# Both borders of a three-sublayer encoder trunk in one ordered list of steps

## The chip, the cores and the metric

One core of one Trainium2 chip runs the kernel. The metric is the device time in microseconds of one execution. A core has five engines with a queue of instructions each: TensorE (PE in the profile; its weight loads are PEld), VectorE (DVE), ScalarE (ACT), GpSimd (POOL) and SyncE (SP), which here only issues DMAs. Each engine runs its own queue in order, and engines wait for one another by semaphores.

## The reference

The kernel computes one layer of three sublayers on x of 512 positions by 1024 features, all in float32:

```python
def sublayer(h_res, j, fn, res_w):
    h = rms_norm(h_res, norm_g[l, 2 * j]) * (1.0 + scale) + shift      # scale, shift, gate: from silu(c) @ w_ada
    y = rms_norm(fn(h), norm_g[l, 2 * j + 1])
    return h_res + res_w * gate * y
...
x = sublayer(x, 0, lambda h: swiglu(h, ffn1_w_in[l], ffn1_w_out[l]), 0.5)     # 1024 -> 2 x 2816 -> 1024
x = sublayer(x, 1, mixer, 1.0)
x = sublayer(x, 2, lambda h: swiglu(h, ffn2_w_in[l], ffn2_w_out[l]), 0.5)
```

The mixer is one input projection, four heads of differential attention with rotary embedding, a bidirectional gated linear recurrence with a short convolution, and one output projection.

## The kernel before

Everything lies transposed: features on the 128 partitions, the 512 positions along the free axis, so x is eight tiles `X[:, k]` of 128x512. Each float32 operand of a product is split into a rounded part and the rest (`h` and `l`, "high" and "low"), and each product is three matmuls (`mm3`, lines 155 to 157): high x high, low weight x high, high weight x low. A weight unit comes by DMA from SP into one of three buffers `st` (`wdma`, L177), ACT copies its high part (`wcopy`, L184: `wh`), and DVE or POOL subtracts it for the low part (`wlow`, L192: `wl`). Each of `st`, `wh` and `wl` has three buffers, so unit i waits for unit i-3.

The two FFNs walk over 44 input tiles (`tile`, eight contraction tiles k each) and then over eight output tiles. The eighth output tile is run in two halves of 256 positions (`last_tile`), so that the work that follows can begin with the first half. What follows is a border between two sublayers:

- the norm of the sublayer's output: a Square of the last tile (L895), two small matmuls against ones (`acc` L901, `norm` L905) and a square root on ACT (L906), giving `s1`;
- the residual: x is multiplied by `s1` (L420 on POOL for k = 2 to 7, L422 on DVE for k = 0 and 1) and the gated output `F[k]` is added (L424, and L455 for whole tiles). The residual is kept scaled by `s1`; the factor is carried along (`old`, L909) and taken out later (`rr`, `restore_x`);
- the next sublayer's first products run on the unnormalized x times the scale column: `u_hi` (ACT L411) and `u_lo` (DVE L414) split it, `do_k` multiplies contraction tile k into seven PSUM banks (21 products of three). `early` runs tile 0 on the first half, `begin` tiles 0 and 1 in halves and 2 and 3 whole, `rest` tiles 4 to 7. `shift_cols` (L397) adds the product with the shift as a column;
- the next pre-norm: Squares of X on ACT (L465) summed by POOL (L467), one matmul pair (`do_stats`, L471 and L472), then variance (L511 or, in the mixer, L999), a square root on ACT, and a reciprocal on DVE (L517, L1009) give `r12`. With it X is normalized (L526, L1013) and split into `R.h`, the input of all further tiles, and the seven first products are scaled when they leave PSUM (L772, L1046).

The order of all this is the order in which the Python code is written (`half`, `early`, `begin`, `rest`, and the start of `ffn` for the second FFN). The mixer between is different: `MIXER` is a list of 565 step names, worked off one after another. Each step is a small function (`xs.0`: first evacuation; `cd.0`, L1301 and L1305: a convolution; `cl.0`, L964: its low part; `ga.00`: its gate product; `sc`, scores; `mo`, `mp`: output projection; a suffix `.p` puts a step on POOL). The list begins with the fifth contraction tile of the mixer's input (`kk.4`) and ends with the sum of the output's squares (`pa.6`), and so contains neither border.

## Time and profile before

| | |
|---|---|
| median of 3 runs | 1009.28 us (1006.93 to 1009.36) |
| profiled execution | 1004.12 us, span 1002.3 us |
| PE busy, 0 to 376 us (first FFN) | 367.73 us |
| PE busy, 376 to 429 us (first border) | 48.78 of 53 us |
| PE busy, 429 to 530 us (mixer, first part) | 93.27 of 101 us |
| PE busy, 530 to 606 us (mixer, rest) | 76.00 of 76 us |
| PE busy, 606 to 670 us (second border) | 57.81 of 64 us |
| PE busy, 670 to 1002 us (second FFN) | 318.21 of 332 us |
| mean granted TensorE clock | 0.989 |

Busy time counts a matmul from its start to its modelled end. The granted clock is the share of full speed that TensorE was allowed; where it is under 1, busy time is slow time. The profiled execution was shorter than the three timed runs.

### The profile page before, as it was taken

How to read it: one execution, taken by the hardware profiler on the slowest of the kernel's cores; microseconds unless marked ns; L12 is line 12 of the kernel's file. 1: busy time of each engine (PE TensorE's matmuls, PEld its weight loads, DVE VectorE, ACT ScalarE, POOL GpSimd, SP SyncE). 2: the span in 40 equal slices, each digit the busy share in tenths (PEclk: the TensorE clock that was granted, in tenths of full speed). 3: DMA queues.
4: the chain of work that ended last, by engine and by line, in shares of the span. 5: the costliest groups of instructions: out<-in, count | busy, mean ns of one | idle time of the engine just before them, and what ended most of it. 6: DMA issues, size and time to landing. Idle time of an engine off the chain costs nothing.

```text
span 1002.3 us, 11743 instructions
## 1 busy us (share of the span) xinstructions
PE 961.8 (96%) x4480; PEld 789.3 (79%) x4480; DVE 608.2 (61%) x789; ACT 430.9 (43%) x666; POOL 222.3 (22%) x163
## 2 busy tenths in 40 slices
PE   6999999999999999979999998999999999999994
PEld 5888888888888888767677788778888888888884
DVE  7967655556666648998998647987433333322226
ACT  6653323335222224689878764363332322222230
POOL 1008200000001015612585416644100000001014
PEclk9999999999999999999999999999999999999997
DMA  8846555455687852322320322314233232333312
GB/s 329 291 154 227 191 192 205 177 208 203 217 276 250 284 168 65 93 74 77 90 75 22 82 81 74 100 64 123 88 105 102 87 105 87 93 95 99 95 37 84
DMA packets 45002, 137.10 MB, mean 137 GB/s; under 512 B 7185, under 2 KB 9745, under 8 KB 44946
## 3 DMA queue, kind: packets, MB, share of 16 engines
q1 hardware_dynamic: 44082, 135.62, 41.1%
q8 instruction: 35, 0.57, 0.2%
q10 hardware_dynamic: 864, 0.74, 0.2%
q14 instruction: 21, 0.17, 0.1%
HBM read 132.14 MB, written 2.10 MB: 134 GB/s over the span
## 4 chain that ended last, share of the span: by engine, by line
PE 84%; DVE 7%; ACT 3%; issue 2%; POOL 2%; DMA 1%; SPq 0%; DVEq 0%; ACTq 0%; POOLq 0%
PE PS L157 27%; PE PS L155 27%; PE PS L156 27%; PE PS L1173 1%; PE PS L702 1%; POOL s L526 1%; DVE X L424 1%; DMA q<-in_w_ada 1%; DVE wl L192 1%; DVE s L1565 1%; ACT s L1186 1%; POOL s L467 1%; DVE s L414 1%; PE PS L1210 1%; DVE X L422 1%
## 5 line engine op out<-in xcount | busy, mean ns | idle before, releaser
L155 PE MATMUL PS<-s,wh 128*128 128x512 f32 (+1 forms) x1032 | 395.8, 384 | 1.9 <-ACT s L411 1.4
L156 PE MATMUL PS<-s,wl 128*128 128x512 f32 (+1 forms) x1032 | 392.4, 380 | 2.9 <-POOL wl L192 1.5
L157 PE MATMUL PS<-s,wh 128*128 128x512 f32 (+1 forms) x1032 | 392.5, 380 | 2.1 <-DVE s L414 2.1
L192 DVE TENSOR_TENSOR wl<-st,wh 128x1024 fp32r<-128x1024 f32 (+3 forms) x151 | 189.0, 1253 | 193.8 <-ACT wh L184 193.6
L155 PEld LDWEIGHTS PS<-s,wh 128*128 128x128 f32 x1032 | 194.3, 188 | 41.7 <-ACT s L411 1.8
L156 PEld LDWEIGHTS PS<-s,wl 128*128 128x128 f32 x1032 | 194.4, 188 | 41.7 <-POOL wl L192 2.4
L157 PEld LDWEIGHTS PS<-s,wh 128*128 128x128 f32 x1032 | 194.3, 188 | 39.8 <-DVE s L414 2.7
L184 ACT ACTIVATE wh<-st 128x1024 fp32r<-128x1024 f32 (+2 forms) x170 | 169.8, 1002 | 120.0 <-PE PS L157 109.0
L155 PE MATMUL PS<-q,wh 128*128 128x512 f32 (+1 forms) x288 | 106.5, 370 | 0.0
L156 PE MATMUL PS<-q,wl 128*128 128x512 f32 (+1 forms) x288 | 106.2, 369 | 0.0
L157 PE MATMUL PS<-q,wh 128*128 128x512 f32 (+1 forms) x288 | 106.0, 368 | 0.0
L879 POOL TENSOR_TENSOR s<-s,s 128x512 f32<-128x512 f32 x12 | 15.7, 1308 | 401.1 <-ACT s L875 401.1
L237 DVE CUSTOM_DVE_ANT_0 q<-q,q 128x1024 bf16<-128x1024 f32 x72 | 89.8, 1247 | 0.2 <-DMA q<-in_w_ada 0.2
L793 DVE TENSOR_TENSOR s<-s,PS 128x512 f32<-128x512 f32 x41 | 28.1, 686 | 62.7 <-PE PS L157 62.1
L788 ACT ACTIVATE s<-PS 128x512 f32<-128x512 f32 x40 | 23.8, 595 | 97.6 <-PE PS L157 97.5
L155 PEld LDWEIGHTS PS<-q,wh 128*128 128x128 f32 x288 | 54.3, 189 | 9.7
L156 PEld LDWEIGHTS PS<-q,wl 128*128 128x128 f32 x288 | 54.2, 188 | 9.6
L157 PEld LDWEIGHTS PS<-q,wh 128*128 128x128 f32 x288 | 54.1, 188 | 9.5
L750 ACT ACTIVATE q<-s 128x512 fp32r<-128x512 f32 x28 | 17.7, 631 | 95.8 <-DVE s L793 94.5
L192 POOL TENSOR_TENSOR wl<-st,wh 128x1024 fp32r<-128x1024 f32 (+2 forms) x18 | 39.6, 2205 | 60.1 <-ACT wh L184 60.1
L750 ACT ACTIVATE s<-s 128x512 fp32r<-128x512 f32 x16 | 10.1, 632 | 70.5 <-DVE s L793 70.5
L751 DVE TENSOR_TENSOR q<-s,q 128x512 fp32r<-128x512 f32 x28 | 22.0, 786 | 20.0 <-ACT q L750 20.0
(235 smaller groups left out, 946.6 us busy)
## 6 DMA issues: line engine op xcount, KB each, us to landing
q<-in_w_ada SPq DMA_DIRECT2D x72, 512.0 KB, 4.0
st<-in_w2b SPq DMA_DIRECT2D x37, 512.0 KB, 3.3
st<-in_w1b SPq DMA_DIRECT2D x36, 512.0 KB, 4.5
st<-in_w1o SPq DMA_DIRECT2D x16, 512.0 KB, 4.4
st<-in_w2o SPq DMA_DIRECT2D x16, 512.0 KB, 3.5
st<-in_wma SPq DMA_DIRECT2D x16, 448.0 KB, 4.2
st<-in_w2a SPq DMA_DIRECT2D x16, 448.0 KB, 3.4
st<-in_wmb SPq DMA_DIRECT2D x9, 512.0 KB, 3.7
```

The lines of the kernel that those rows point to most:

```text
L155: PE.matmul(o, wh, ah, start=start, stop=False)
L156: PE.matmul(o, wl, ah, start=False, stop=False)
L157: PE.matmul(o, wh, al, start=False, stop=stop)
L184: ACT.activation(h[:, :n], staged[i][:, :n], AF.Copy)
L192: eng.tensor_tensor(out=l[:, :n], in0=st[:, :n], in1=h[:, :n].bitcast(F32), op=ALU.subtract)
L237: DVE.tensor_tensor_reduce(out=junk, in0=t, in1=cond, op0=ALU.mult, op1=ALU.add, scale=1.0, scalar=0.0, accum_out=ada[:, i:i + 1])
L414: DVE.scalar_tensor_tensor(out=ul[k][:, c], in0=X[:, k, c], scalar=colA(j, k), in1=f32(uh[k][:, c]), op0=ALU.mult, op1=ALU.subtract)
L750: ACT.activation(h, t, AF.Copy)
L751: DVE.tensor_tensor(out=l, in0=t, in1=f32(h), op=ALU.subtract)
L788: ACT.activation(t, PS[:, b], AF.Silu)
L793: DVE.tensor_tensor(out=g, in0=g, in1=PS[:, b], op=ALU.mult)
L879: POOL.tensor_tensor(out=st["acc"], in0=st["acc"], in1=t, op=ALU.add)
```

## The change

Both borders become steps of the list, which grows from 565 to 878 names and now runs from the last output tile of the first FFN (`ws.-5`, `pt.1.0.0`) to the second of the two input tiles after the second FFN's first seven (`tt.8.1`). The functions `half`, `early`, `begin` and `rest` go, and `last_tile` serves only the last sublayer; each instruction of the borders is a step with the border's number (1 or 2), the half (0, 1) and the tile k: `pt` (part of the last output tile), `qs` (its Square), `sa` and `sn` (the norm's matmuls), `sq` (square root), `so` (product of the carried factors), `xm` (x times `s1`, a half), `xf` and `xg` (the added output, half and whole), `uh` and `ul` (the split), `kq` and `kk` (products of contraction tiles 0 and 1 in halves, and of the rest), `sx` and `sax` (Square and sum), `e2` (epsilon term), `sh` and `sw` (shift), `ss` (matmuls of the sum), `hm`, `hf`, `hh`, `hl` (normalized input), `sg`, `sl`, `pg`, `ph`, `pl` (the second FFN's first groups), `tt` (its next two tiles). The steps inside the mixer keep their instructions, but the whole list stands in another order, and which of the steps run on POOL is chosen anew. The side work of the first FFN is packed into 57 places instead of 60.

```diff
 MIXER = """
-wd.2 ws.2 kk.4 kk.5 gh.1 wd.3 gh.0 sd sf sr rv hm.0 ws.3 hf.0 wl.2 hm.2 wl.3 hm.7 hh.0 hm.6 dq hl.0 wd.4 kk.6
...
+ws.-5 lt.1 dq pt.1.0.0 sa.1.0 wl.-5.p pt.1.0.1 pt.1.0.2 pt.1.1.0 qs.1.0 sn.1.0 pt.1.1.1 pt.1.1.2 wd.-4 wd.-3
...
-        def half(F, s1, c):
-
-            for k in range(2, 8):
-                POOL.tensor_tensor(out=X[:, k, c], in0=X[:, k, c], in1=s1[:, c], op=ALU.mult)
-            for k in range(2):
-                DVE.tensor_tensor(out=X[:, k, c], in0=X[:, k, c], in1=s1[:, c], op=ALU.mult)
-            for k in range(2):
-                DVE.tensor_tensor(out=X[:, k, c], in0=X[:, k, c], in1=F[k][:, c], op=ALU.add)
-                u_hi(k, c)
-            for k in range(2):
-                u_lo(k, c)
...
+        def xm(e, b, h, k):
+            c = HF[h]
+            e.tensor_tensor(out=X[:, k, c], in0=X[:, k, c], in1=B["s1", 1][:, c], op=ALU.mult)
+
+        def xf(e, b, h, k):
+            c, f = HF[h], ST[b]["F"][k]
+            e.tensor_tensor(out=X[:, k, c], in0=X[:, k, c], in1=f[:, c], op=ALU.add)
...
+        def sax(e, b, k):
+            t, o = B.pop(("sx", b, k)), B["sx", b, 0]
+            e.tensor_tensor(out=o, in0=o, in1=t, op=ALU.add)
...
-    def mixer(R, s1, nxt, early):
-        base = pos["i"]
+    def trunk(st0, part0, done0, side3, finish, last):
+
+        base = pos["i"] + 7
...
-        for i in range(60):
+        for i in range(57):
...
-        G = group0(1, 7)
-        st = ffn(0, R, side2, step(G), G.early)
...
-        G.begin(st["F"], st["s1"])
...
-        R, G = G, group0(2, 7)
-        st = mixer(R, st["s1"], step(G), G.early)
...
-        G.begin(st["F"], st["s1"])
...
-        G.rest(2)
...
+        st = next(ffn(0, R, side2))
...
+        trunk(st, st["part"], st["done"], side3, finish, last)
```

Three places show how the instructions move. A row names the line, the operation, what it writes and reads (a number tells buffers apart) and the size; `x4` is four in a row. On DVE at the first border, from the last weights of the first FFN (768 wide) on, there stood before:

```order
L192 TENSOR_TENSOR wl<-st,wh 128x768
...
L422 TENSOR_TENSOR X<-X,s_2635 128x256 x2
L424 TENSOR_TENSOR X<-X,s_1991 128x256
L424 TENSOR_TENSOR X<-X,s_2101 128x256
L414 SCALAR_TENSOR_TENSOR s_2754<-X,aA,s_2753 128x256
L414 SCALAR_TENSOR_TENSOR s_2758<-X,aA,s_2757 128x256
L192 TENSOR_TENSOR wl<-st,wh 128x896 x2
```

Now, with L891 for `xm`, L214 for a weight's low part, L438 for `ul` and L901 for `xg`:

```order
L214 TENSOR_TENSOR wl<-st,wh 128x1024
L891 TENSOR_TENSOR X<-X,s_2645 128x256 x4
L214 TENSOR_TENSOR wl<-st,wh 128x896 x2
L438 SCALAR_TENSOR_TENSOR s_2805<-X,aA,s_2804 128x256
L438 SCALAR_TENSOR_TENSOR s_2814<-X,aA,s_2813 128x256
L891 TENSOR_TENSOR X<-X,s_2645 128x256 x3
L901 TENSOR_TENSOR X<-X,s_2212 128x512
```

The mixer's first two weights moved ahead of the low inputs, the half sums of k = 0 and 1 left DVE, and more of the half products came to it; the 768-wide low part went to POOL. On DVE at the mixer's start, where the first groups leave PSUM, there stood before (L1046 evacuates, L1301 and L1305 are a convolution, L964 its low part):

```order
L1046 TENSOR_TENSOR s_3174<-PS,s_2849 128x512
L1046 TENSOR_TENSOR s_3185<-PS,s_2849 128x512
L1301 TENSOR_SCALAR s_3188<-q_3055,par 128x512
L1305 SCALAR_TENSOR_TENSOR s_3188<-q_3055,par,s_3188 128x510
L1305 SCALAR_TENSOR_TENSOR s_3188<-q_3055,par,s_3188 128x511 x2
L1301 TENSOR_SCALAR s_3208<-q_3055,par 128x512
L1305 SCALAR_TENSOR_TENSOR s_3208<-q_3055,par,s_3208 128x510
L1305 SCALAR_TENSOR_TENSOR s_3208<-q_3055,par,s_3208 128x511 x2
L964 TENSOR_TENSOR s_3224<-s_3188,s_3223 128x512
```

Now (L1019, L1274 and L1278, L811):

```order
L1019 TENSOR_TENSOR s_3185<-PS,s_3057 128x512
L1019 TENSOR_TENSOR s_3188<-PS,s_3057 128x512
L1019 TENSOR_TENSOR s_3192<-PS,s_3057 128x512
L1274 TENSOR_SCALAR s_3206<-q_3066,par 128x512
L1278 SCALAR_TENSOR_TENSOR s_3206<-q_3066,par,s_3206 128x510
L1278 SCALAR_TENSOR_TENSOR s_3206<-q_3066,par,s_3206 128x511 x2
L1274 TENSOR_SCALAR s_3220<-q_3066,par 128x512
L1278 SCALAR_TENSOR_TENSOR s_3220<-q_3066,par,s_3220 128x510
L1278 SCALAR_TENSOR_TENSOR s_3220<-q_3066,par,s_3220 128x511 x2
L811 TENSOR_TENSOR s_3212<-s_3206,s_3211 128x512
```

One evacuation more stands ahead of the two convolutions, and the low part still stands behind both. On POOL at the second border, from the weights of the last mixer tiles to those of the second FFN, there stood before:

```order
L192 TENSOR_TENSOR wl<-st,wh 128x896
L420 TENSOR_TENSOR X<-X,s_2635 128x256 x12
L467 TENSOR_TENSOR s_4826<-s_4826,s_4915 128x512
...
L490 TENSOR_TENSOR s_4827<-s_4711 128x512
L491 TENSOR_SCALAR s_4827<-s_4827 128x512
L526 TENSOR_TENSOR s_5032<-X,s_4828 128x512
...
L192 TENSOR_TENSOR wl<-st,wh 128x1024 x4
```

Now (L1444 is `pa`, L895 `xf`, L811 the low part of a normalized input):

```order
L214 TENSOR_TENSOR wl<-st,wh 128x896
L1444 TENSOR_TENSOR s_4586<-s_4586,s_4700 128x512
L1444 TENSOR_TENSOR s_4586<-s_4586,s_4704 128x512
L895 TENSOR_TENSOR X<-X,s_4589 128x256
L214 TENSOR_TENSOR wl<-st,wh 128x896 x2
L811 TENSOR_TENSOR s_5141<-s_5071,s_5140 128x512
...
L214 TENSOR_TENSOR wl<-st,wh 128x1024 x3
```

The twelve half products, the six sums of squares (L467), the epsilon steps and the five normalizing products (L526) left POOL for DVE; four input splits and two weights' low parts came.

## The prediction

> **What bounds the kernel now.** I read the page's busy shares first, then the busy time by stretches of 10 us, then what TensorE waited for, then the timeline of each engine at the waits.

> ```profile
> PE 961.8 (96%) x4480; PEld 789.3 (79%) x4480; DVE 608.2 (61%) x789; ACT 430.9 (43%) x666; POOL 222.3 (22%) x163
> ```

> ```profile
> 370.00:380.00 10.00, 10.00 (x82) 9.84 (x81) 3.30 (x5) 1.95 (x5) 3.26 (x4) 1.00 0.53 144
> 380.00:390.00 10.00, 7.85 (x62) 7.39 (x61) 8.40 (x10) 4.82 (x9) 6.41 (x8) 1.00 0.29 92
> 400.00:410.00 10.00, 8.17 (x33) 5.76 (x33) 10.00 (x9) 8.73 (x13) 8.24 (x6) 1.00 0.19 52
> 410.00:420.00 10.00, 10.00 (x46) 8.27 (x45) 8.75 (x9) 3.94 (x6) 5.71 (x3) 1.00 0.43 136
> 420.00:430.00 10.00, 8.76 (x39) 6.93 (x37) 8.74 (x15) 8.86 (x14) 2.48 (x1) 1.00 0.36 114
> 430.00:440.00 10.00, 6.00 (x19) 4.56 (x20) 9.93 (x14) 7.71 (x12) 4.31 (x2) 0.83 0.00 0
> 480.00:490.00 10.00, 9.44 (x46) 6.76 (x44) 9.90 (x11) 9.24 (x15) 7.11 (x5) 1.00 0.33 95
> 490.00:500.00 10.00, 8.40 (x39) 5.95 (x40) 9.39 (x11) 6.89 (x15) 4.84 (x3) 1.00 0.21 63
> 510.00:520.00 10.00, 9.73 (x52) 6.54 (x52) 9.52 (x15) 8.01 (x18) 7.41 (x6) 1.00 0.34 105
> 550.00:560.00 10.00, 10.00 (x49) 6.92 (x49) 6.77 (x14) 8.76 (x21) 7.58 (x7) 1.00 0.21 53
> 610.00:620.00 10.00, 7.19 (x52) 6.32 (x52) 8.35 (x12) 3.79 (x8) 8.48 (x10) 1.00 0.08 32
> 630.00:640.00 10.00, 8.13 (x32) 5.58 (x30) 10.00 (x9) 6.08 (x10) 8.49 (x6) 0.95 0.18 53
> 640.00:650.00 10.00, 10.00 (x40) 7.96 (x39) 8.23 (x6) 2.43 (x3) 5.08 (x4) 0.88 0.49 150
> 660.00:670.00 10.00, 8.49 (x37) 6.38 (x36) 7.61 (x9) 7.91 (x11) 6.07 (x3) 1.00 0.26 84
> ```

> The columns are the stretch, its length, busy time of PE, PEld, DVE, ACT and POOL, the granted clock, DMA share and GB/s. TensorE is the bound, so only its idle time can be won. In the part that the change rewrites it idles 2.15 + 1.83 us at the first border, 1.24 + 4.00 at the mixer's start, 0.56 + 1.60 + 0.27 inside the mixer and 2.81 + 1.87 + 1.51 at the second border: 17.8 us. The clock adds some: busy time by the missing share is 1.0 us in 430 to 440 (6.00 x 0.17), 0.4 in 630 to 640 and 1.2 in 640 to 650. At most 20.4 us are to be had, 2% of the time.

> ```profile
> PE PS L157 <- DVE s L964: 4.0, 1, 4.0
> PE PS L471 <- POOL s L467: 3.7, 2, 1.9
> PE PS L157 <- DVE s L414: 2.1, 3, 0.7
> PE PS L156 <- POOL wl L192: 1.5, 1, 1.5
> PE PS L156 <- DVE wl L192: 1.4, 1, 1.4
> ```

> These are the waits by releaser (total, times, longest). None is for a DMA; each is for elementwise work that came late, on DVE or POOL.

> **First border.** The same matmuls run, 82 of 256 columns in 10 us (0.12 us each), 46 of 512 (0.22 each). What moves is the work beside them.

> ```profile
> 376.70 1.31 DVE L422 TENSOR_TENSOR X<-X,s 128x256 f32<-128x256 f32 x2 [7.85 <-ACT s L906]
> 376.74 5.38 POOL L420 TENSOR_TENSOR X<-X,s 128x256 f32<-128x256 f32 x6 [8.38 <-ACT s L906]
> 381.45 2.62 DVE L192 TENSOR_TENSOR wl<-st,wh 128x896 fp32r<-128x896 f32 x2
> 380.20 1.78 ACT L184 ACTIVATE wh<-st 128x896 fp32r<-128x896 f32 x2
> 381.89 0.36 ACT L895 ACTIVATE s<-PS 128x256 f32<-128x256 f32 x1
> 404.55 3.10 POOL L467 TENSOR_TENSOR s<-s,s 128x512 f32<-128x512 f32 x2 [0.27 <-ACT s L465]
> 377.93 1.83 DVE L424 TENSOR_TENSOR X<-X,s 128x256 f32<-128x256 f32 x2
> 608.44 0.43 DVE L909 TENSOR_TENSOR s<-s,s 128x256 f32<-128x256 f32 x1 [0.98 <-ACT s L906]
> 622.03 1.28 DVE L455 TENSOR_TENSOR X<-X,s 128x512 f32<-128x512 f32 x2
> 631.00 3.37 POOL L467 TENSOR_TENSOR s<-s,s 128x512 f32<-128x512 f32 x2 [2.97 <-ACT s L465]
> 631.51 1.70 DVE L455 TENSOR_TENSOR X<-X,s 128x512 f32<-128x512 f32 x1
> ```

> Before, ACT splits the first mixer weights (380.20) only behind the first products' inputs, so their low parts start at 381.45 and TensorE waits 1.4. Now ACT does both copies right behind the square root of the first half, near 377; DVE has four half products (up to 0.92 each beside POOL, as 1.83 for two shows: 3.7), two low parts (2.6) and one low input ahead, from 376.7, and ends near 384. TensorE has then the second norm and the 14 shift matmuls, which used to stand behind the first products, and needs that input at about 384: the wait is gone. New is that it stands empty for the Square of the second half (0.36 plus the handover, 0.45 together), which the first products used to cover.

> Squares: POOL summed six (3.10 for two) and TensorE waited 1.9 for the last; now DVE sums five of six at 0.64 (1.28 for two), and POOL one. POOL's halves fall from twelve to six, so DVE runs at 0.43 a half instead of up to 0.92. DVE gains nine half products and five sums (7.1 us), loses three half sums (1.3) and two 896-wide low parts, and each half that no longer runs beside POOL gives back some 0.4 to 0.5. The products on the first four contraction tiles cover that: 84 of 0.12 and 42 of 0.22, 19 us. I take 3.98 - 0.45 = **3.5 us** won; ends 1.5 (half the sums late) and 4.0.

> **Mixer's start.** The gates need a convolution's low part.

> ```profile
> 424.71 1.37 DVE L1046 TENSOR_TENSOR s<-PS,s 128x512 f32<-128x512 f32 x2 [1.00 <-PE PS L157]
> 426.20 0.55 DVE L1301 TENSOR_SCALAR s<-q,par 128x512 f32<-128x512 f32 x1
> 426.78 2.33 DVE L1305 SCALAR_TENSOR_TENSOR s<-q,par,s 128x510 f32<-128x510 f32 x3
> 429.02 0.54 DVE L1301 TENSOR_SCALAR s<-q,par 128x512 f32<-128x512 f32 x1
> 431.51 2.62 POOL L192 TENSOR_TENSOR wl<-st,wh 128x1024 fp32r<-128x1024 f32 x1 [5.53 <-ACT wh L184]
> 431.84 2.84 DVE L964 TENSOR_TENSOR s<-s,s 128x512 fp32r<-128x512 f32 x1
> 432.60 1.28 ACT L1359 ACT_TABLE_LOAD   x1
> ```

> From the first evacuation to the end of that low part (424.71 to 434.68) DVE took 10.0 us while TensorE had six tiles, 3.9 us, left. In the new order still two convolutions (2.8 each, 426.20 to 429.02) stand ahead of it, and three evacuations instead of two: 2.0 + 5.6 + 0.7 = 8.3 us if the low part does not meet POOL, as it met the step of 431.51. So this gap stays: 8.3 - 3.9 - 0.45 (two matmuls between) = 3.9 of 5.24 us, and DVE is idle ahead of it. With half of the slow clock's 1.0 that is **1.8 us** won; ends -1 (the low part again 2.8) and 4.

> [...]

> **Inside the mixer** the list is another one with the same steps. DVE, at 9.4 to 9.9 of 10, is the partner that TensorE waits for at 480 to 520 (2.43 us). More of the input's low parts go to POOL, fewer stand ahead of the first scores. Two more table loads (1.28 each) fall late, where ACT has room (8.76 of 10 with TensorE full); uncovered they cost up to 2.6. I take half of the 2.43, **1.2 us**; ends -4 (new waits the size of the old ones, and both loads) and 2.4.

> SP's loads and rotation copies keep their relation: no weight load stands ahead of a rotation copy while its buffer is still in use. I cost that at nothing; TensorE has no DMA among the waits above.

> **Second border.**

> ```profile
> 645.95 8.90 POOL L526 TENSOR_TENSOR s<-X,s 128x512 f32<-128x512 f32 x5 [4.92 <-DVE s L517]
> 659.64 2.52 POOL L192 TENSOR_TENSOR wl<-st,wh 128x1024 fp32r<-128x1024 f32 x1 [4.79 <-ACT wh L184]
> ```

> POOL loses twelve half products, six sums, the two steps for the epsilon term and five normalizing products (8.90 us), and keeps one half sum, two low parts of weights and four of inputs. DVE takes twelve half products more (5.2 at 0.43), the sums (3.8), five products (3.2) and the epsilon steps (about 1.3): 13.5 us; it hands over two 896-wide low parts and four input splits (about 4.7). Twelve half steps that ran at 0.65 to 0.92 beside POOL run at 0.43 (some 4 us back) and a 512-wide sum at 0.64, not 1.70, as beside the POOL step of 631.00. So DVE is not later than before. The sum of squares now comes after one full contraction tile instead of two, which takes 4.6 us (21 x 0.22) of its cover; that is the lower end. And the second FFN's first weight tile is split by DVE, ahead of the last input splits, not by POOL at 659.64. New: two waits of 0.45 for Squares, since both norms stand right behind their halves. 6.19 + 1.6 (clock) - 0.9 = **6.9 us**; ends 3 and 7.8.

> **Sum.** 3.5 + 1.8 + 1.2 + 6.9 = 13.4 us. The profiled execution took 1004.1 (span 1002.3 and 1.8 around it), so it would be 990.7; the runs' median, 1009.3, lies 5.2 above, and the difference carried over gives 996.

> **Rivals.** *Mixer pays back*: the new order brings waits of 6 to 9 us at the gates and scores, where DVE is full. Against it stands that fewer splits are ahead there; 1003. *Nothing to measure*: it also eats the first border; 1009. *DVE becomes the bound at the second border* and the kernel is slower: if the 13.5 us ran beside POOL at 0.92 a half and 1.70 a full step (11.0 + 10.2 + 8.5 + 2.5 = 32 us), they would exceed DVE's idle time (1.65 + 0 + 1.77 in the quoted stretches) and the 4.7 handed over by over 20 us; the gain is lost once some 13 of these are uncovered, and at 20 the time is 1016. Against it: POOL has one half step there until the low parts. [...] *More*: the gates' wait goes too; 989.

> Chances: forecast (986 to 1000) 0.65, pays back 0.14, more 0.05, nothing 0.08, slower 0.08. A change under 0.3% (3 us) can't be told from none. Faster 0.84, same 0.08, slower 0.08. The range, 988 to 1004, reaches to the paid-back case.

> **What would show it.** Right: POOL nearly idle between the half norms of the second border, half-width DVE steps at 0.43, no TensorE wait for the sum of squares nor for a weight's low part, a wait of 3 to 4 us for the convolution's low part still there. Wrong: idle stretches of TensorE of over 2 us where the scores or the rotated q and k are due, or half steps near 0.9.

## The result and the profile after

The changed kernel takes 985.82 us (median of 4 runs, 984.59 to 986.26), the kernel before on the same chip 1008.11 (4 runs, 1005.25 to 1009.36): a ratio of 0.9777, 95% interval 0.9755 to 0.9799, so 22.3 us less. The prediction said 996 with 988 to 1004: the direction was right, the size too small, and the time lies below the range. Its profiled execution took 985.61 us (span 983.8). The page's busy shares:

```profile
PE 957.7 (97%) x4480; PEld 789.3 (80%) x4480; DVE 595.8 (61%) x814; ACT 432.3 (44%) x668; POOL 201.2 (20%) x138
```

VectorE does 25 instructions more than before and is busy 12 us less; GpSimd does 25 fewer. TensorE's waits (total, times, longest) in the rewritten part:

```profile
PE PS L179 <- DVE s L811: 2.6, 1, 2.6
PE PS L177 <- ACT s L1301: 1.8, 1, 1.8
PE PS L1146 <- DVE q L811: 0.4, 1, 0.4
```

Only the gates' wait is left (L1301 is `ch`, L811 under it `cl`), and 0.4 us at the scores. By stretches of 10 us (length, busy PE, PEld, DVE, ACT, POOL, granted clock, DMA share, GB/s):

```profile
380.00:390.00 10.00, 9.96 (x81) 9.51 (x81) 10.00 (x16) 6.55 (x12) 5.66 (x5) 1.00 0.32 93
420.00:430.00 10.00, 6.55 (x27) 4.63 (x26) 8.80 (x13) 8.73 (x15) 3.81 (x2) 0.90 0.32 106
430.00:440.00 10.00, 8.98 (x32) 7.30 (x33) 9.89 (x15) 9.69 (x16) 3.38 (x3) 0.76 0.13 33
490.00:500.00 10.00, 10.00 (x58) 7.97 (x56) 9.94 (x18) 7.61 (x18) 5.62 (x4) 1.00 0.31 112
610.00:620.00 10.00, 10.00 (x59) 8.44 (x58) 9.83 (x16) 6.63 (x11) 0.00 (x0) 1.00 0.14 47
```

Both borders are full (9.96 and 10.00 where 7.85 and 7.19 stood; no stretch from 370 to 420 or from 590 to 670 is under 9.96). The only large hole is the gates', 420 to 440, with a clock of 0.90 and 0.76 behind it. At the second border, on VectorE and GpSimd (start, us, engine, line, operation, in brackets the idle time ahead and what ended it):

```profile
599.28 1.43 DVE L891 TENSOR_TENSOR X<-X,s 128x256 f32<-128x256 f32 x4
604.38 0.85 POOL L895 TENSOR_TENSOR X<-X,s 128x256 f32<-128x256 f32 x1 [9.85 <-DVE X L891]
615.45 1.48 DVE L925 TENSOR_TENSOR s<-s,s 128x512 f32<-128x512 f32 x2
622.77 2.72 POOL L214 TENSOR_TENSOR wl<-st,wh 128x896 fp32r<-128x896 f32 x1 [17.54 <-ACT wh L206]
```

GpSimd has one step from 594.5 to 622.8. Four half products on VectorE take 1.43 and two sums 1.48, so 0.36 and 0.74 each where 0.43 and 0.64 were forecast.

Where the time went is read from the starts of TensorE's instructions in the traces: a stage lasts from its first product to the next stage's (the first border to the last of the mixer's first products, `gm.1.6`). Gains in us, against the first profile of the kernel before (the prediction's) and against a second one, which was taken with the experiments:

| term | forecast | first profile | second profile |
|---|---|---|---|
| start-up and first FFN | 0 | -1.3 | -1.4 |
| first border | 3.5 | 4.4 | 4.4 |
| mixer's start (gates' waits, slow clock there) | 1.8 | 0.2 | 0.6 |
| inside the mixer | 1.2 | 5.9 | 8.0 |
| second border and the FFN behind | 6.9 | 9.3 | 11.7 |
| sum | 13.4 | 18.5 | 23.2 |

The first row says little of the change. In a second profile of the changed kernel the first FFN ended at 364.60 us and not at 365.66; in the two profiles of the kernel before it ended at 364.36 and 364.23.

### The profile page after: what moved, and what is told of

It reads as the page before. It is cut to its first block, busy times and chain, and to the rows that moved or that the text cites. A ratio compares the mean times of both kernels' runs of the same rounds, so it can differ in the third digit from the quotient of the medians.

```text
span 983.8 us, 11742 instructions
## 1 busy us (share of the span) xinstructions
PE 957.7 (97%) x4480; PEld 789.3 (80%) x4480; DVE 595.8 (61%) x814; ACT 432.3 (44%) x668; POOL 201.2 (20%) x138
## 4 chain that ended last, share of the span: by engine, by line
PE 94%; DVE 4%; DMA 1%; SPq 0%; issue 0%; ACT 0%; DVEq 0%; ACTq 0%
PE PS L177 30%; PE PS L179 30%; PE PS L178 30%; PE PS L1146 1%; PE PS L1183 1%; DVE s L1574 1%; DVE s L1577 1%; DMA X<-in_xT 1%; DVE s L1278 0%; PE PS L1219 0%; DVE s L1569 0%; PE PS L1237 0%; PE PS L476 0%; PE PS L419 0%; PE PS L872 0%; SPq L465 0%
## 5 line engine op out<-in xcount | busy, mean ns | idle before, releaser
L214 DVE TENSOR_TENSOR wl<-st,wh 128x1024 fp32r<-128x1024 f32 (+3 forms) x148 | 178.4, 1207 | 191.0 <-ACT wh L206 190.8
L206 ACT ACTIVATE wh<-st 128x1024 fp32r<-128x1024 f32 (+2 forms) x170 | 170.3, 1002 | 127.7 <-PE PS L179 115.1
L214 POOL TENSOR_TENSOR wl<-st,wh 128x1024 fp32r<-128x1024 f32 (+3 forms) x21 | 50.7, 2422 | 61.0 <-ACT wh L206 61.0
L625 ACT ACTIVATE q<-s 128x512 fp32r<-128x512 f32 x24 | 15.2, 632 | 95.4 <-DVE s L654 95.4
L414 DVE SCALAR_TENSOR_TENSOR s<-st,ada,s 128x512 f32<-128x512 f32 (+1 forms) x28 | 19.7, 743 | 26.6 <-DMA st<-in_wma 13.4
```

What stands on the lines that cost most here:

```text
L206: ACT.activation(h[:, :n], staged[i][:, :n], AF.Copy)
L214: eng.tensor_tensor(out=l[:, :n], in0=st[:, :n], in1=h[:, :n].bitcast(F32), op=ALU.subtract)
L414: DVE.scalar_tensor_tensor(out=o, in0=i, scalar=colS(j, k), in1=o, op0=ALU.mult, op1=ALU.add)
L625: ACT.activation(h, t, AF.Copy)
```

## Experiments

All ran beside the kernel before on the same chip. They ran in three groups on three chips, on which the kernel before had medians of 1007.72, 1007.63 and 1007.54 us; so kernels derived from the changed one are held against its 984.97 us of the first group. Where the list has fewer or more lines, line numbers shift by a few.

**The changed kernel again, and the kernel before again.** The same files, no edit.

> The changed kernel once more, to know its spread and that of the kernel before. If the gain is waits that are gone, each execution gains it: 985 to 987 us, all within 0.2%, and the kernel before 1005 to 1009.5 again. If a part of the 22 us by medians is the luck of single executions (the profiled one before took 1004.1), the changed kernel spreads as far as the one before, 985 to 989.

> The kernel before with a second profile. Theory (a wait of TensorE costs its length and, in most executions, some slow clock behind it, and the first profile was an execution with little of that): a span of 1004.5 to 1008 us at a granted clock of 0.984, the same waits to 0.2 us, and a clock of 0.7 to 0.9 in stretches behind waits where the first profile had 1.00. Rival (the waits themselves vary): the clock as in the first profile and a wait that is 2 us longer.

Measured: the changed kernel 984.97 us (984.56 to 986.6, 5 runs); the kernel before 1008.7 (1005.32 to 1010.76, 8 runs), profiled at a span of 1007.0, 4.7 longer than the first profile, granted clock 0.984 instead of 0.989. Its stretches:

```profile
430.00:440.00 10.00, 6.03 (x18) 4.52 (x19) 9.93 (x14) 7.72 (x12) 4.30 (x2) 0.66 0.00 0
490.00:500.00 10.00, 8.63 (x33) 5.93 (x34) 9.38 (x11) 6.97 (x15) 4.75 (x3) 0.81 0.26 76
610.00:620.00 10.00, 8.10 (x49) 7.43 (x48) 6.41 (x10) 2.60 (x6) 6.06 (x7) 0.83 0.24 83
660.00:670.00 10.00, 7.12 (x25) 5.16 (x24) 8.41 (x12) 8.28 (x11) 3.56 (x2) 0.84 0.15 52
```

The first profile had 0.83, 1.00, 1.00 and 1.00 there. The wait at the scores is the same (1.64 us against 1.68 by starts), but behind it 12 matmuls take about 0.43 us instead of 0.23, some 2.45 us in all; in the first profile, whose clock there is 1.00, none did. Not all is clock: at the end of the second border the waits differ too (1.5 us for a weight's low part in the first profile; 2.1, and 0.8 for its high part, in the second).

Finer stretches show how the clock falls. In these traces it is either 1.00 or 0.50, and it is 0.50 for 3.41 us or a multiple of that. Leaving out the start and the last 12 us, the first profile has two such slow slices of 3.41 us, the second six. At a clock of 0.50 a slice can cost at most half its length, 1.7 us by my estimate. The same two waits at the second border (1.4 and 0.9 us by starts), in the first profile and (behind the dots) in the second:

```profile
608.22:611.63 3.41, 2.23 (x18) 1.97 (x16) 3.15 (x5) 0.70 (x2) 2.68 (x4) 1.00 0.56 177
611.63:615.04 3.41, 2.69 (x18) 2.43 (x19) 2.04 (x3) 1.41 (x4) 2.64 (x4) 1.00 0.02 5
...
612.23:615.64 3.41, 1.51 (x10) 1.10 (x10) 3.41 (x5) 1.65 (x4) 3.41 (x5) 1.00 0.24 98
615.64:619.05 3.41, 3.41 (x16) 3.23 (x15) 0.68 (x2) 0.47 (x1) 0.96 (x2) 0.50 0.02 5
```

The edges of the slow slices lie on one grid of 3.41 us through each execution. In the first profile an edge parts the two waits, and TensorE is busy for 2.23 and 2.69 us of the slices on its two sides; in the second both waits lie in one slice, TensorE is busy for 1.51 of its 3.41 us, and the next slice is slow. In all fourteen traces, cut along this grid from 30 us on, each of the 32 full-clock slices in which TensorE was busy for a share of 0.45 or less was followed by a slow one, and none with a share of over 0.60 was. Between the two both occur, and the wait at the scores lies there (0.59 in the first profile, 0.60 in the second).

Over the executions of the kernel before that ran beside the last experiments, spans go with the clock: 1003.4 and 1003.6 at 0.987 and 0.990, 1003.9 to 1007.6 at 0.984 and 0.985, 1008.2 to 1008.8 at 0.980 and 0.982. The first profile (0.989, 1002.3) was one of the few with little slow clock.

**The other half of that: TensorE kept busy in its waits.** In the changed kernel:

```diff
+                fill(8)                       # PE.matmul(PS[:, z], gh_, R.h[1][0]), first gate product only
                 PE.matmul(o, gh_, h, start=True, stop=False)
                 PE.matmul(o, gl_, h, start=False, stop=False)
+                fill(11)
                 PE.matmul(o, gh_, l, start=False, stop=True)
```

> The changed kernel with 19 more matmuls (512 columns, their result is never read) where TensorE waits at the gates: 8 ahead of the first gate product and 11 ahead of its third matmul, 1.8 and 2.5 us in waits of 2.0 and 2.95. They add nothing to the output. Theory (the clock falls because TensorE stood idle): the granted clock stays 1.00 from 420 to 440, the 7 to 9 matmuls that took 0.43 take 0.22, 1.4 to 2 us faster than the changed kernel, 983 to 983.8 us, and less spread. Rival (the clock falls for another reason, or the filling matmuls end late): 985 to 986.5 us.

Measured: 983.08 us (982.31 to 983.71, 4 runs), 1.9 less than the changed kernel in its own five runs (ratios to the kernel before 0.9754, 0.9733 to 0.9774, and 0.9772, 0.975 to 0.9795).

```profile
420.00:430.00 10.00, 9.97 (x45) 7.86 (x43) 8.78 (x13) 9.14 (x15) 3.79 (x2) 1.00 0.32 106
430.00:440.00 10.00, 9.69 (x43) 7.77 (x42) 9.89 (x15) 9.41 (x15) 3.04 (x3) 1.00 0.19 46
```

The gates come no sooner, but the clock stays at 1.00: 1.9 us of slow clock hung on 5 us of waits. In the kernel before, 16 such matmuls at the gates and 6 ahead of the scores' wait at 493:

```diff
+                    for _ in range(16):
+                        PE.matmul(PS[:, z], gh_, R.h[0][0], start=True, stop=True)
...
+            for _ in range(6 if n == 7 else 0):
+                PE.matmul(PS[:, b[0]], qs[0][:, c], ks[0], start=True, stop=True)
```

> The kernel before with 22 more matmuls of 512 columns where TensorE waits, their result overwritten or never read: 16 (3.6 us) in the gates' wait of 4.15, 6 (1.4 us) in the scores' wait of 1.64 us at 493. Theory (the slow clock behind these waits, 1.0 to 1.4 us at the gates and 0.3 to 2.45 at the scores, is what most timed executions of the kernel before have over the first profiled one): 1003.5 to 1005.5 us against some 1007.6, and a smaller spread. Rival (the executions differ elsewhere): 1007 to 1009 us.

Measured: 1006.07 us (1003.89 to 1007.99, 12 runs), ratio 0.9983 (0.9969 to 0.9996).

```profile
430.00:440.00 10.00, 9.48 (x40) 7.54 (x41) 9.93 (x13) 8.55 (x14) 4.37 (x2) 1.00 0.00 0
490.00:500.00 10.00, 9.80 (x47) 6.98 (x46) 9.38 (x11) 6.85 (x15) 4.89 (x3) 1.00 0.22 70
```

The clock holds at both places, but the kernel gains 1.5 us and not the 2 to 4 expected, and still varies by 4 us. So these two places carry only a part; the waits at the borders, which were not filled, keep theirs (the trace still has 0.87 from 640 to 650). And what TensorE saves behind the gates it waits for soon after: at 444.35 it stands for 1.5 us until ScalarE (L1369) has emptied a bank, where it stood for 0.3 at 444.36 in the first profile. ScalarE comes no sooner, so faster matmuls gain little there.

**Mixer's start: the chain to the first gate brought forward.** In the changed kernel:

```diff
- xs.0 xa.0 xs.1 hf.1.5 hf.1.6 kfree.1 xs.2 gm.1.4 gm.1.5 xa.1 hh.1.6 xa.2 hf.1.0 cd.0 ch.0 hh.1.0 hh.1.3 cd.2 hh.1.2 wl.4.p hh.1.7 ch.2 cl.0 xs.3
+ xs.0 xa.0 xs.1 hf.1.5 hf.1.6 kfree.1 cd.0 gm.1.4 gm.1.5 hh.1.6 xs.2 ch.0 xa.1 xa.2 hf.1.0 cl.0 cd.2 hh.1.0 hh.1.3 hh.1.2 wl.4.p hh.1.7 ch.2 xs.3
```

> The changed kernel with five names of the list moved: the first convolution cd.0 stands ahead of the third evacuation xs.2, its rounded copy ch.0 ahead of xa.1 on ScalarE, and its low part cl.0 ahead of the second convolution cd.2. Theory (the gates wait for one chain, xs.0 xa.0 cd.0 ch.0 cl.0, in which VectorE and ScalarE put other work): the chain ends 2.5 to 3 us earlier, the waits at the gates fall from 5.3 to 2 to 3 us, the slow clock behind them shrinks, 982 to 983.5 us. Rival (VectorE is full from 413 to 440 us of the span, so what is moved back is missed a little later): the input's low parts come as much later as the gates come earlier, 985 to 986 us.

Measured: 982.87 us (982.72 to 983.9, 5 runs), 2.1 less than the changed kernel beside it; the ratio to the kernel before is 0.9751 (0.9729 to 0.9773). It is the fastest ordering tried, and within 0.3 us of the filled one. Its waits and stretches:

```profile
PE PS L175 <- ACT s L1299: 2.6, 2, 1.6
```

```profile
420.00:430.00 10.00, 7.47 (x31) 5.22 (x29) 8.91 (x14) 8.71 (x15) 2.52 (x2) 1.00 0.22 76
430.00:440.00 10.00, 9.27 (x37) 6.75 (x38) 9.89 (x15) 9.97 (x17) 3.47 (x3) 1.00 0.16 39
```

The wait is split: 1.06 for `ch.0` and 1.56 for `ch.2`, and the clock stays at 1.00 behind both. A part of the win was paid back, as the rival said: the second convolution is now what comes late.

**Inside the mixer: the order of before between the new borders.** From `gm.1.6` to `pf.0` the steps stand as before, with their engines:

```diff
- gm.1.6 hh.1.5 wd.7 rs.k0 hh.1.4 hl.1.0 ga.00 gs.00 rs.q1 hl.1.1 ra.q0 ga.01 rd.q0 cd.1 ...
+ gm.1.6 hl.1.0 hh.1.5 hh.1.4 cd.1 ga.00 ch.1 rs.k0 gs.00 wd.7 rs.q1 cl.1 ga.01 gs.01 wl.5.p ...
```

> The changed kernel up to its last first-group product (gm.1.6) and from the second border on (pf.0), and between them the steps in the order and on the engines of the kernel before. Theory (the order inside the mixer carries some 6 us, as waits that are gone and as score products that no longer lie apart): 991 to 993 us, waits of TensorE of 2 us and more inside the mixer again, the 96 score products at about 18 us by their starts, not 14. Rival (the mixer gained because the border before it ends earlier and with less left to do, whatever the order inside): 985.5 to 987.5 us.

Measured: 997.72 us (993.07 to 998.99, 4 runs), 12.7 above the changed kernel, twice what the theory gave.

```profile
PE PS L177 <- DVE s L809: 3.2, 2, 2.8
PE PS L1144 <- ACT s L1157: 1.4, 1, 1.4
```

```profile
490.00:500.00 10.00, 8.58 (x33) 5.89 (x33) 9.38 (x11) 7.08 (x16) 4.65 (x3) 0.79 0.25 70
```

The waits at the scores are back, with the slow clock, and one more: 2.6 us at a gate product (433.5 by starts), since this order was written behind another mixer's start. By starts the mixer takes 180.0 us from its first gate; with the new order 167.0, in the kernel before 173.3 and 175.8. The order inside carries a large part, but 4 to 7 of the 12.7 belong to the misfit of the two halves.

**Inside the mixer: one step of the kernel before moved.** In its trace, around the scores, TensorE first:

```profile
487.19 0.76 PE L1173 MATMUL PS<-s,s 64*128 64x512 f32 x4
488.42 1.56 PE L1173 MATMUL PS<-s,s 64*128 64x512 f32 x8 [0.47 <-DVE s L1147]
489.91 0.50 PE L155 MATMUL PS<-s,wh 128*128 128x512 f32 x1
...
493.32 0.50 PE L1173 MATMUL PS<-s,s 64*128 64x512 f32 x1
495.22 2.12 PE L1173 MATMUL PS<-s,s 64*128 64x512 f32 x11 [1.41 <-ACT s L1186]
497.53 0.50 PE L155 MATMUL PS<-s,wh 128*128 128x512 f32 x1 [0.20 <-ACT s L1186]
...
493.10 1.28 ACT L1186 ACT_TABLE_LOAD   x1 [3.82 <-DVE sm L1180]
...
489.47 2.40 POOL L192 TENSOR_TENSOR wl<-st,wh 128x1024 fp32r<-128x1024 f32 x1
...
489.49 2.93 DVE L1389 TENSOR_TENSOR q<-s,q 128x512 f32<-128x512 f32 x1
492.34 2.47 DVE L1180 TENSOR_REDUCE sm<-PS 128x1 f32<-128x512 f32 x4
```

TensorE waits for score banks; ScalarE frees them with the exponentials, for which it stands idle 3.82 us until VectorE has the maxima (L1180); these stand behind a product (L1389, `lm.21`) that takes 2.93 us beside GpSimd. The edit to the kernel before:

```diff
- vl.1 ws.12 lm.21 mx.6 ex.6 wl.11.p zF.k1 mx.4
+ vl.1 ws.12 mx.6 ex.6 wl.11.p zF.k1 mx.4 lm.21
```

> The kernel before with one name moved: lm.21, a product of 512 columns that takes 2.93 us beside GpSimd, stands behind the softmax maxima mx.6 and mx.4, not ahead of them. ScalarE waited 3.82 us for these maxima, and TensorE for the score banks that ScalarE frees. Theory (this one place carries most of what the mixer gains inside): the score waits at 487 to 497 (0.5 to 1.9 us each, some 4 us) and the slow clock behind them go, 1002.5 to 1005 us. Rival (the gain is spread over many places, and the maxima wait for the next thing): 1006.5 to 1008 us.

Measured: 1003.25 us (1000.9 to 1007.71, 12 runs), ratio 0.9954 (0.9939 to 0.9969): 4.3 us for one name.

```profile
491.75 2.48 DVE L1179 TENSOR_REDUCE sm<-PS 128x1 f32<-128x512 f32 x4 [0.46 <-PE PS L1172]
494.15 1.25 DVE L1388 TENSOR_TENSOR q<-s,q 128x512 f32<-128x512 f32 x1
...
492.52 1.28 ACT L1185 ACT_TABLE_LOAD   x1 [1.51 <-DVE sm L1179]
```

ScalarE now waits 1.51, the product takes 1.25, and no wait over 0.3 us is left at this place but the first (0.47, for VectorE's low part). So one place carries most of what the mixer gains inside: 4.3 us by medians, of 5.9 to 8.0 by the traces.

**Score halves in another order.**

```diff
-            for i, (x, y) in enumerate(((0, 0), (0, 1), (1, 0))):
-                for m, part in ((0, lo), (1, hi)):
+            for m, part in ((0, lo), (1, hi)):
+                for i, (x, y) in enumerate(((0, 0), (0, 1), (1, 0))):
```

> The changed kernel with the six matmuls of a score block in another order: first the three on the lower 64 rows, then the three on the upper 64, so that only one neighbouring pair of a block is on different rows, not five. Theory (neighbours on different halves of the rows run side by side, and the new list's gain inside the mixer is partly that waits no longer stand between them): the 96 score matmuls take 19 to 21 us by their starts, not 14, and the kernel 990 to 992 us. Rival (the short starts are an accident of the queue, work is the same): 985 to 986 us.

Measured: 985.32 us (984.11 to 986.43, 4 runs), no difference; the 96 score matmuls take 13.9 us by starts in both. Two blocks, in the changed kernel and (second fence) here:

```profile
457.01 1.66 PE L1146 MATMUL PS<-s,s 64*128 64x512 f32 x12
458.60 0.50 PE L177 MATMUL PS<-wh,s 128*128 128x512 f32 x1
```

```profile
457.84 1.67 PE L1146 MATMUL PS<-s,s 64*128 64x512 f32 x12
459.44 0.50 PE L177 MATMUL PS<-wh,s 128*128 128x512 f32 x1
```

My theory fell: the order in which the kernel writes them does not matter. The trace starts these matmuls in pairs either way: 44 of the 48 are at most 0.010 us apart in the changed kernel and 42 in the kernel before, most of them 0.003 or 0.004; 0.010 here. It does not show which rows a started matmul lies on, so a pair may still be one of the lower and one of the upper half. In the kernel before the 96 take 18.4 us; the 4.5 between that and 13.9 are its waits.

**Inside the mixer: the engines of before.** 21 names of the changed list get the engine they had, the order stays:

```diff
- zC.k0.p lg.11.p lg.20 ... lm.30 lf.0.p ll.2.p lf.1.p w1.13 w1.15
+ zC.k0 lg.11 lg.20.p ... lm.30.p lf.0 ll.2 lf.1 w1.13.p w1.15.p
```

> The changed kernel, its order kept, with the engine of before for the 21 steps inside the mixer whose choice of VectorE or GpSimd differs. Theory (order carries the mixer's gain): 985 to 986.5 us. Rival (which engine takes which step does): 988 to 991 us.

Measured: 1005.71 us (1003.91 to 1006.43, 10 runs), 20.7 more than the changed kernel: nearly the whole change, and far outside both expectations.

```profile
PE PS L1144 <- DVE s L809: 8.6, 1, 8.6
```

```profile
540.09 2.48 POOL L1360 TENSOR_TENSOR q<-s,q 128x512 f32<-128x512 f32 x2 [6.27 <-ACT s L1348]
542.53 1.26 POOL L1372 TENSOR_TENSOR q<-q,q 128x512 f32<-128x512 f32 x1
...
543.83 1.73 DVE L1391 TENSOR_TENSOR q<-q,s 128x512 f32<-128x512 f32 x1 [7.14 <-POOL q L1372]
```

`lm.30`, now on GpSimd (L1360), waits there 6.27 us for ScalarE's square root. Behind it in that queue stands `la.0` (L1372), and `lf.0` (L1391), now on VectorE, waits for that one: VectorE idles 7.14 us, with the low parts of the last scores' inputs behind it, and TensorE 8.6. In the changed kernel `lf.0` waited on GpSimd, where nothing urgent was behind it. By the starts of TensorE, matmul for matmul against the changed kernel, the mixer loses 19.7 us: 8.8 in this wait, 4.6 in shorter ones (2.7 at 484 and 1.9 at 461 to 463 us, at earlier scores), and 6.0 in slow clock, which is granted at 0.50 from 486.0 to 492.9 and from 544.1 to 554.3. So the largest single loss is a step that waits, put into the wrong queue; that this step alone would cost as much was tested by no run.

**Second border: engine and order apart.** First the new order with the engines of before, 24 steps:

```diff
- xm.2.0.4 ... xm.2.1.7 sax.2.1 ... sax.2.6 e2.2 hm.2.1 ...
+ xm.2.0.4.p ... xm.2.1.7.p sax.2.1.p ... sax.2.6.p e2.2.p hm.2.1.p ...
```

> The changed kernel with the second border's engines as before: the half products of k = 2 to 7, the sums of squares, the epsilon step and five normalizing products go to GpSimd, 24 steps, and the order stays. Theory (it is the engine: GpSimd is slower and slows VectorE beside it): half steps near 0.9 us, the wait for the sum of squares is back with 2 us and more, 990 to 996 us. Rival (it is the order, which serves the first contraction tiles first): 985.5 to 988 us.

Measured: 994.18 us (993.66 to 994.97, 4 runs), 9.2 above the changed kernel.

```profile
PE PS L177 <- DVE s L436: 2.9, 2, 2.6
```

```profile
609.85 6.93 POOL L923 TENSOR_TENSOR s<-s,s 128x512 f32<-128x512 f32 x4
608.07 4.06 DVE L899 TENSOR_TENSOR X<-X,s 128x512 f32<-128x512 f32 x3
```

The whole-tile additions on VectorE (L899) take 1.35 each beside GpSimd's half products and sums of squares, which take 0.96 and 1.73; in the changed kernel one alone (606.45) took 0.68. GpSimd's half products take 0.86 to 0.96, as expected, but the wait is for a low input (L436, `ul`), not for the sum of squares. Then the engines of the new kernel in the order of before:

```diff
-            for k in range(2, 8):
-                POOL.tensor_tensor(out=X[:, k, c], in0=X[:, k, c], in1=s1[:, c], op=ALU.mult)
...
+            if j == 2:
+                scale(DVE, range(2, 8))        # behind the two u_lo; sums, epsilon step and do_m likewise on DVE
```

> The kernel before with the second border's half products of k = 2 to 7, sums, epsilon step and five normalizing products on VectorE, in the order of before (the half products behind the first inputs' low parts). The other half of e_b2_pool. Theory (the gain of the second border needs engine and order together, since e_b2_pool lost 9 of its 9.3 us): TensorE's waits there fall by 2 to 5 us, 1002 to 1006 us. Rival (the engine alone carries it): 7 us and more, 998 to 1001 us. Second rival (on VectorE in the old order they come late): 1008 to 1014 us.

Measured: 1005.25 us (1002.55 to 1007.76, 10 runs), ratio 0.9972 (0.9957 to 0.9987).

```profile
PE PS L475 <- DVE s L471: 3.7, 1, 3.7
```

The waits for the first products go, but the sum of squares now comes later (3.7 us, 1.9 before). So the engine alone gives 2.4 us. The new order alone leaves the changed kernel 9.2 us slower, so it gives next to nothing of the 9.3 us against the first profile, and 2.5 of the 11.7 against the second.

**First border: the weights split late, as before.**

```diff
- wd.-2 ws.-4 ws.-3 xm.1.0.2 ... xf.1.0.1.p wl.-4 qs.1.1 uh.1.0.1 wl.-3 ... ul.1.0.1
+ wd.-2 xm.1.0.2 ... xf.1.0.1.p qs.1.1 uh.1.0.1 ws.-4 ws.-3 ... ul.1.0.1 wl.-4 wl.-3
```

> The changed kernel with the mixer's first two weight units split late at the first border, as before: their copies behind the inputs' high parts, their low parts behind the inputs' low parts. Theory (the split ahead of the inputs is worth the wait of 1.4 to 1.6 us that stood there): a wait for a weight's low part is back, 986.2 to 987.5 us. Rival (the norm and the shift matmuls that now stand ahead of the first products cover it): 985 us.

Measured: 986.32 us (985.12 to 987.09, 4 runs), 1.35 more, with runs that overlap those of the changed kernel (984.56 to 986.6); the border itself is 0.9 longer by starts.

```profile
PE PS L176 <- DVE wl L212: 0.3, 1, 0.3
```

The second norm and the shift matmuls cover most of the old wait of 1.4; the early split saves what is left, 0.9 by the trace. No run tests the rest of the first border's 4.4 by itself.

## Why the prediction was too small

The forecast gain of 13.4 fell short of 22.3 by 8.9 us. Of these, 4.7 are the term inside the mixer, 2.4 the second border and 0.9 the first; the mixer's start and the first FFN took back 1.6 and 1.3; and 3.8 lie between the profiled difference and that of the medians.

**The pool was measured with the wrong ruler.** I took TensorE's idle time from busy time by stretches: 17.8 us, and 20.4 with the clock as a ceiling. But a matmul of 512 columns is shown busy for 0.39 us while the next starts after 0.23, so the first 0.16 of every wait count as busy. At the scores it is more: the two pairs of blocks quoted above from the kernel before take 489.91 - 487.19 = 2.72 and 497.53 - 493.32 = 4.21 us where an undisturbed pair takes 458.60 - 457.01 = 1.59, so 3.75 us are lost there, and busy time showed 2.16 of them (0.56 + 1.60 in 480 to 500). The changed kernel won 18.5 of a "ceiling" of 20.4 and still has 5 us of waits. Busy time misleads here by hiding a part of each wait (1.59 of the 3.75 us at the scores), and it is the measure on which my sum stood.

**Inside the mixer: 1.2 forecast, 5.9 measured.** "I take half of the 2.43" had no row behind it. The chain `lm.21`, maxima, exponentials, score banks was in the profile shown before, and I had not followed it: one name is worth 4.3 us by medians. This is the step that failed most: I took half of 2.43 us of idle time, and did not work out what made it and what would go with it. That low parts of the input moved to GpSimd, my reason, was tested by no run.

**Second border: 6.9 forecast, 9.3 measured.** The mechanism held: half steps at 0.43 and below, no wait for the sum of squares nor for a weight's low part, GpSimd nearly idle. The size went wrong by the ruler: the waits were 7.8 us by starts and not 6.19. The slow clock was one slice of 3.41 us, so at most 1.7, near the 1.6 taken; the two norms standing in front cost about 1.0, near the 0.9 taken. The remaining 0.8 of the 9.3 is in short gaps. That DVE would become the bound is refuted by 9.83 of 10 busy with TensorE full; e_b2_pool shows the rival's price where GpSimd is used: 1.35 for a whole-tile addition that took 0.68 alone.

**First border: 3.5 forecast, 4.4 measured,** above the upper end of 4.0, by the same ruler: the waits that went are 1.6, 0.9 and 2.0 us by starts. The Square wait is there (0.5 together with the norm). The weights' early split is worth 0.9 to 1.35, not the 1.4 to 1.6 that I gave it.

**Mixer's start: 1.8 forecast, 0.2 measured.** I wrote that 3.9 us would stay "if the low part does not meet POOL". It met it:

```profile
429.08 1.33 POOL L811 TENSOR_TENSOR s<-s,s 128x512 fp32r<-128x512 f32 x1 [6.19 <-ACT s L993]
429.20 1.76 DVE L811 TENSOR_TENSOR s<-s,s 128x512 fp32r<-128x512 f32 x1
```

1.76 us beside GpSimd; with the chain brought forward it took 0.69 alone. That is 1.07 more, and the waits came to 5.0 by starts, against 5.6 before. I had also counted half of the slow clock's 1.0 as won. Instead the slow clock there lasted 6.83 us and not 3.41, and matmuls behind the gates lose 1.8 us to it where they lost 1.4: 0.6 won and 0.4 lost. The rival *more* (the gates' wait goes too) did not happen either: the kernel fell below its 989 with that wait in place.

**The carried difference.** I subtracted the profiled difference from the median. The execution profiled before had a clock of 0.989 where most have 0.984 or less, and so lay 3.5 to 5 us below the median; the changed kernel has fewer waits, and its profile equals its runs (985.61 and 985.82). With these waits went the slow clock behind them, of which the execution profiled before had little (two slow slices, the second profile six). This fits the 3.8 us between 18.5 and 22.3; the second profile of before makes it 23.2. The filled kernels show the clock's part directly (1.9 and 1.5 us); of the 4.7 us between the two profiles, four more slow slices, at most 1.7 us each, can be the whole, but the waits that differ have a part that was not split off.

The slow slices of 3.41 us lie on a grid that started elsewhere in the two executions profiled before (an edge at 608.22 in the first profile, at 612.23 in the second), and the same two waits at the second border were followed by no slow slice where an edge parted them and by one where both lay in one slice. TensorE did not have to stand idle for a whole slice: two in which it was still busy for 1.51 and 2.04 of 3.41 us (612.23 and 492.77 in the second profile) were followed by a slow one.

Rivals: *mixer pays back*, *nothing*, and *slower* are refuted by the stages' lengths.

## What to carry to other kernels

Measure what TensorE can win from the starts of its matmuls, not from its busy time, and follow each wait back through the other engines before putting a number on it. Here a wait cost its length and, where it left TensorE busy for a share of 0.45 or less of a 3.41 us slice (32 slices in fourteen traces), a slow slice behind it, at most 1.7 us each by the estimate above; so compare clocks before carrying a profile's difference to a median. Engine and order are one choice: moving 21 steps to other engines without moving their places cost 20.7 us, most of it in waits behind steps that now stood in another queue and in the slow clock behind these waits.
